# A transformer trunk's first feed-forward: its first two column groups interleaved by quarters of x, and the transfers of x set between those of the weights

## The chip, the cores and the metric

One core of a Trainium2 chip runs the whole program. The metric is the device time of one execution in microseconds; lower is better. TensorE (PE) does matrix products into the accumulation memory PSUM, with weight loads (PEld) beside them; VectorE (DVE), ScalarE (ACT) and GpSimd (POOL) work element by element; SyncE (SP) issues the transfers (DMA). Each engine works through its own queue in order.

## The reference

Two layers, each with a feed-forward, a mixing stage of three branches, and a second feed-forward. The change touches the first feed-forward of the first layer alone:

```python
def _swiglu(u, wi, wo):
    a, g = jnp.split(u @ wi, 2, axis=-1)
    return (jax.nn.silu(a) * g) @ wo

for l in range(DEPTH):
    x = x + 0.5 * _swiglu(_rms_norm(x, ffn1_norm[l]), ffn1_wi[l], ffn1_wo[l])
    ...
```

x has 256 tokens and 1024 features, `wi` is 1024 x 2816 and `wo` 1408 x 1024, all in float32.

## The kernel before

Every float32 operand is split into a high and a low part, and a product of two is done as three (high x high, high x low, low x high). For a weight tile, ACT casts the raw tile to the high part (`conv_hi`), and DVE subtracts it from the raw one for the low part (`conv_lo`). In the trace raw tiles are `raw`, and high and low parts are `whi` and `wlo` or, in another ring of buffers, two tiles `g`. There are four raw buffers (`RAW`); SP issues the transfer of a further tile where a low part has been issued and so releases a buffer.

The normalised x is used in a raw form first: x^T times the gain, as `uh` (high, ACT) and `ul` (low, DVE). The factor 1/rms of each token comes later, as a row `rrow` (`rows_of`). x arrives in four quarters of 256 features, two feature tiles of 128 each. In `first_norm` each quarter, in the trace `R`, is transposed on PE into an `at` tile (four products with the identity), and `raw_u` makes its two tiles of `uh` and then of `ul`.

The first feed-forward's up projection goes by column groups of 256 + 256 columns (`plan_ffn`): group c accumulates u @ wi over eight feature tiles k, with the weights of one group in tiles of one or two feature tiles. Such a group needs an accumulator of two PSUM banks (`big_ps`, kind `mm`); there are two of these. One feature tile is two units of six products (`feat_units`). When a group is done, `side_feat` multiplies the accumulator's first half by `rrow` (DVE), applies silu (ACT), multiplies by the accumulator's second half (DVE), gives the accumulator back, and splits the result.

The order of instructions is not written out. `drive` goes through the units in order; before each, `feed` issues weight casts and transfers, and `run_sides` advances the side works (`first_norm`, `side_feat`, and constants in `setup_late`), all by the estimates of `Flow`, which keeps a time for each engine. The engines' queues are then fixed, and semaphores hold them to the data.

The start of the program: in `setup` SP's queue gets quarter 0 of x, two weight tiles, quarter 1, a weight tile, quarter 2, a weight tile, quarter 3. PE does seven warm-up products on a tile of zeros, transposes quarter 0 and the gain, and does four more.

Of the kernel before, what the change touches and what calls it, by code (L numbers as in the profile page):

```python
# [18 lines left out]
P = 128  # L19
# [53 lines left out]
class WTile:  # L73
    """A weight tile: where it comes from, how it lies, and once loaded its hi and lo parts."""
# [8 lines left out]
class Flow:  # L83
    """Estimates when each engine is done with what it was given and when each piece of a tile is ready.

    Engines work in the order in which they are given instructions; the estimates choose that order, and
    the semaphores of the framework keep it right whatever the times turn out to be."""

    LAT, GRAN, COLD = 0.2, 64, 7.0
    TABLES = {AF.Exp: "natural_log_exp_and_others", AF.Ln: "natural_log_exp_and_others",  # L90
# [47 lines left out]
    def note(self, eng, op, args, kw):  # L138
        outs = [args[0]] + [kw[k] for k in ("accum_out",) if k in kw]
        ins = [x for x in (*args[1:], *(v for k, v in kw.items() if k != "accum_out")) if hasattr(x, "tensor")]  # L140
        start, known = self.t[eng], []
# [12 lines left out]
        if eng == "d":  # L154
# [3 lines left out]
            end = max(start, issue + 1.0) + size / 360e3  # L158
# [43 lines left out]
class Trunk:  # L202
    TAIL = 5
    RING, XRING, RAW, WARM = 5, 4, 4, (7, 4)
# [55 lines left out]
    def take(self, kind, shape=None, dt=F32):  # L260
        """a tile of a kind that is given back by hand"""
# [32 lines left out]

    def hook(self, u, *gens):
        self.hooks.setdefault(u, []).extend(gens)

# [7 lines left out]
    def able(self, since, wait):  # L305
        """wait: an engine ("p", "a", "v") and tiles that it reads, (kind, n) for slots, conditions, a time"""
# [32 lines left out]

    def dma_tile(self, i):  # L340
        w = self.tiles[i]
        w.raw = self.tile(self.wp, [P, 1024], "raw", self.RAW)
# [16 lines left out]
    def feed(self, u, urgent=False):  # L359
        """convert weight tiles ahead of unit u as the engines have time, and fetch further ones."""  # L360
# [37 lines left out]
    def drive(self):  # L398
        self.live, self.pend, self.nconv = {"m": [], "x": []}, [], 0
        for u, (w, emit, post, need, reads) in enumerate(self.units):  # L400
            for g in self.hooks.get(u, ()):
                self.spawn(g)
# [19 lines left out]
    def setup(self, N):  # L422
# [20 lines left out]
        for n in range(4):  # L443
            ns = slice(n * 256, (n + 1) * 256)
            nc.sync.dma_start(xt[:, :, ns], a["x"][0, :, ns].rearrange("(t p) c -> p t c", p=P))
            for _ in range((2, 1, 1, 0)[n]):
                self.dma_tile(self.ndma)
                self.ndma += 1
# [14 lines left out]
    def first_norm(self, N, xt, grow, pw, warm_up):  # L463
        nc = self.nc
# [1024 lines left out]
```

## Time and profile before

| | us |
|---|---|
| timed executions, median of 3 (lowest to highest) | 831.48 (831.39 to 831.77) |
| span of the profiled execution, first to last instruction | 829.8 |
| PE busy | 822.6 (99%) |
| DVE busy | 585.0 (70%) |
| ACT busy | 453.7 (55%) |
| share of PE in the chain that ended last | 98% |

The page gives no time of its own for the profiled execution beside the span; the timed executions are 1.7 us longer than it. Times in the rows below count from the span's start. A row of the timeline merges instructions of one kind: where it begins, how long the merged stretch is, how many there are (x4), and in brackets how long the engine was idle before and what ended that. Busy shares of PE are close to full nearly everywhere, since the ends of products are modelled; idle time on PE is read from the brackets and from the distance between starts.

### The profile page before, as it was taken

The numbers are of one execution on the slowest core, as the hardware profiler recorded it, in microseconds if no ns is written. First come the engines' busy times: TensorE is split into PE (matmuls) and PEld (weight loads), VectorE is DVE, ScalarE is ACT, GpSimd is POOL, SyncE is SP. The second block draws the span as 40 slices with busy tenths as digits, with TensorE's granted clock in tenths as the row PEclk, the third lists the DMA queues.
The fourth block names the chain that finished last, engine by engine and source line by source line (L and its number), as shares of the span: only waits on it lengthen the run. The fifth ranks groups of instructions, "written<-read, shape, count | busy, mean of one in ns | idle before, by whom it ended". The sixth has DMA issues, their size and how long they took to land.

```text
span 829.8 us, 16152 instructions
## 1 busy us (share of the span) xinstructions
PE 822.6 (99%) x6459; PEld 793.3 (96%) x6459; DVE 585.0 (70%) x939; ACT 453.7 (55%) x720; POOL 34.7 (4%) x49
## 2 busy tenths in 40 slices
PE   8999999999999999999999999999999999999998
PEld 6999999898999999999999999998989999999996
DVE  5787878987757488855775567898957475886541
ACT  6456545557775446644654444565676745655430
POOL 0000010200300000000000000101002000000000
PEclk9999999999999999999999999999999999999999
DMA  8678735643265746865567555366423655477521
GB/s 259 184 244 256 240 103 158 184 148 103 85 201 155 247 155 205 275 186 172 172 212 203 177 159 165 98 208 185 138 82 115 222 174 186 158 240 242 182 69 51
DMA packets 122255, 145.15 MB, mean 175 GB/s; under 512 B 7534, under 2 KB 97084, under 8 KB 122180
## 3 DMA queue, kind: packets, MB, share of 16 engines
q1 hardware_dynamic: 122020, 144.05, 56.2%
q8 instruction: 50, 0.82, 0.4%
q14 instruction: 25, 0.20, 0.1%
q10 hardware_dynamic: 160, 0.07, 0.0%
HBM read 143.05 MB, written 1.05 MB: 174 GB/s over the span
## 4 chain that ended last, share of the span: by engine, by line
PE 98%; DMA 1%; SPq 0%; DVE 0%; issue 0%
PE mm L188 65%; PE at L188 33%; DMA R<-in_x_dram 1%; DMA raw<-in_ffn_wi_dram 0%; SPq L188 0%; DVE xn L188 0%
## 5 line engine op out<-in xcount | busy, mean ns | idle before, releaser
L188 ACT CAST whi<-raw 128x1024 fp32r<-128x1024 f32 (+3 forms) x185 | 189.9, 1034 | 159.9 <-PE mm L188 58.5
L188 DVE TENSOR_TENSOR wlo<-raw,whi 128x1024 fp32r<-128x1024 f32 (+3 forms) x185 | 220.1, 1199 | 73.9 <-ACT whi L188 73.0
L188 PE MATMUL mm<-uh,whi 128*128 128x256 f32 x840 | 240.2, 286 | 0.0
L188 PE MATMUL mm<-uh,wlo 128*128 128x256 f32 x840 | 236.9, 282 | 0.0
L188 PE MATMUL mm<-ul,whi 128*128 128x256 f32 x840 | 236.4, 281 | 0.0
L188 PEld LDWEIGHTS mm<-ul,whi 128*128 128x128 f32 x840 | 158.8, 189 | 0.1
L188 PEld LDWEIGHTS mm<-uh,whi 128*128 128x128 f32 x840 | 158.0, 188 | 0.5 <-issue 0.3
L188 PEld LDWEIGHTS mm<-uh,wlo 128*128 128x128 f32 x840 | 157.9, 188 | 0.0
L188 PE MATMUL mm<-uh,g 128*128 128x256 f32 x752 | 138.9, 282 | 0.0
L188 ACT CAST g<-raw 128x1024 fp32r<-128x1024 f32 (+3 forms) x87 | 88.2, 1018 | 90.1 <-PE mm L188 35.3
L188 DVE TENSOR_TENSOR g<-raw,g 128x1024 fp32r<-128x1024 f32 (+3 forms) x87 | 102.4, 1183 | 22.4 <-ACT g L188 22.2
L188 PEld LDWEIGHTS mm<-uh,g 128*128 128x128 f32 x752 | 117.5, 188 | 0.0
L188 PE MATMUL mm<-ul,g 128*128 128x256 f32 x376 | 105.6, 281 | 0.0
L188 PE MATMUL at<-R,whi 128*128 128x256 f32 x404 | 71.9, 280 | 0.0
L188 PEld LDWEIGHTS mm<-ul,g 128*128 128x128 f32 x376 | 70.9, 188 | 0.0
L188 PE MATMUL at<-R,g 128*128 128x256 f32 x570 | 69.8, 280 | 0.0
L188 PEld LDWEIGHTS at<-R,g 128*128 128x128 f32 x570 | 68.2, 188 | 0.0
L188 PEld LDWEIGHTS at<-R,whi 128*128 128x128 f32 x404 | 61.6, 188 | 0.0
L188 PE MATMUL at<-R,wlo 128*128 128x256 f32 x202 | 56.3, 279 | 0.0
L188 PEld LDWEIGHTS at<-R,wlo 128*128 128x128 f32 x202 | 38.1, 189 | 0.0
L188 DVE TENSOR_TENSOR R<-s2k,R 128x512 fp32r<-128x512 f32 (+1 forms) x24 | 15.5, 647 | 25.7 <-ACT R L188 25.7
L188 PE MATMUL mm<-whi,uh 128*128 128x512 f32 (+1 forms) x76 | 30.0, 394 | 0.0
(229 smaller groups left out, 1150.0 us busy)
## 6 DMA issues: line engine op xcount, KB each, us to landing
raw<-in_w_in_dram SPq DMA_DIRECT2D x92, 512.0 KB
raw<-in_ffn_wi_dram SPq DMA_DIRECT2D x174, 256.0 KB
raw<-in_ffn_wo_dram SPq DMA_DIRECT2D x35, 512.0 KB
raw<-in_w_out_dram SPq DMA_DIRECT2D x16, 512.0 KB
raw<-in_ffn_wo_dram SPq DMA_DIRECT2D x12, 384.0 KB
raw<-in_w_up_ml_dram SPq DMA_DIRECT2D x16, 256.0 KB
raw<-in_w_in_dram SPq DMA_DIRECT2D x8, 424.0 KB
raw<-in_w_up_sb_dram SPq DMA_DIRECT2D x8, 256.0 KB
```

What stands on the lines that cost most here:

```text
L188: f(*args, **kw)
```

## The change

In the first feed-forward of the program, groups 0 and 1 are planned together: for each quarter of x, the four units of group 0 on it and then the four units of group 1 (`reorder`). All later groups are as before. The transfers of x are put before given weight tiles (`X_BEFORE`): quarter 0 ahead of tile 0, quarter 1 ahead of tile 3, quarter 2 ahead of tile 4, quarter 3 ahead of tile 5; those ahead of tiles 4 and 5 are thus issued when these tiles are. A quarter's transposes wait until the plan is at unit 8q - 3, that is, after the first of group 1's units on the quarter before. In quarter 0 the second feature tile of `uh` and `ul` waits for the first weight cast. Two warm-up products take the place of four, and the estimates take a lower rate for the first transfers. (The file also loses its comments, which shifts its line numbers.)

```diff
@@ class Flow @@
+    FIRST_RATE, FIRST_US = 240e3, 12.0
...
-            end = max(start, issue + 1.0) + size / 360e3
+            end = max(start, issue + 1.0) + size / (self.FIRST_RATE if issue < self.FIRST_US else 360e3)
@@ class Trunk @@
-    RING, XRING, RAW, WARM = 5, 4, 4, (7, 4)
+    RING, XRING, RAW, WARM = 5, 4, 4, (7, 2)
+    X_BEFORE = {0: 0, 3: 1, 4: 2, 5: 3}
...
+    def reorder(self, units):
+        self.units, self.tiles = [], []
+        for w, *_ in units:
+            w.first = None
+        for x in units:
+            self.unit(*x)
...
+    def dma_x(self, n):
+        ns = slice(n * 256, (n + 1) * 256)
+        self.nc.sync.dma_start(self.xt[:, :, ns], self.a["x"][0, :, ns].rearrange("(t p) c -> p t c", p=P))
+
     def dma_tile(self, i):
         w = self.tiles[i]
+        if i in self.X_BEFORE:
+            self.dma_x(self.X_BEFORE[i])
...
         for u, (w, emit, post, need, reads) in enumerate(self.units):
+            self.at_unit = u
@@ setup @@
-        for n in range(4):
-            ns = slice(n * 256, (n + 1) * 256)
-            nc.sync.dma_start(xt[:, :, ns], a["x"][0, :, ns].rearrange("(t p) c -> p t c", p=P))
-            for _ in range((2, 1, 1, 0)[n]):
-                self.dma_tile(self.ndma)
-                self.ndma += 1
+        self.xt = xt
+        for _ in range(self.RAW):
+            self.dma_tile(self.ndma)
+            self.ndma += 1
@@ first_norm @@
         for q in range(4):
+            yield lambda: self.at_unit >= 8 * q - 3,
             yield "p", xt[:, :, 256 * q:256 * q + 256], self.ident, ("ps", 1)
...
             yield "a", pt
-            self.raw_u(N, q, v)
+            if q == 0:
+                self.raw_u(N, q, v, (0,))
+                yield lambda: self.nconv > 0,
+                self.raw_u(N, q, v, (1,))
+            else:
+                self.raw_u(N, q, v)
@@ plan_ffn @@
-        for c in range(5):
+        start, c0 = not self.units, 0
+        if start:
+            c0, parts = 2, []
+            for c in range(2):
+                box = {}
+                first = len(self.units)
+                self.feat_units(tiles(256 * c, 256, (0, 1, 2, 4, 6, 8) if c == 0 else (0, 2, 4, 6, 8)), 4, U, box,
+                                lambda b=box, c=c: self.spawn(side_feat(b, 2 * c, 2)), key="n")
+                parts.append(self.units[first:])
+            self.reorder([x for q in range(4) for p in parts for x in p[4 * q:4 * q + 4]])
+        for c in range(c0, 5):
             box = {}
-            cuts = (0, 1, 2, 4, 6, 8) if not self.units else (0, 2, 4, 6, 8)
-            self.feat_units(tiles(256 * c, 256, cuts), 4, U, box,
+            self.feat_units(tiles(256 * c, 256, (0, 2, 4, 6, 8)), 4, U, box,
                             lambda b=box, c=c: self.spawn(side_feat(b, 2 * c, 2)), key="n")
```

How this moves instructions is shown at three places.

**DVE at the program's start.** Names: `at` an x quarter transposed, `gain` the norm's gain, `g` with an odd first number a weight tile's low part (written from the raw tile and the high part). Before:

```order
L188 COPY gain_20_116<-mm_17_106 128x8
L188 SCALAR_TENSOR_TENSOR ul_115<-at_21_117,gain_20_116,uh_114 128x256 x2
L188 TENSOR_TENSOR g_1_24_138<-raw_87,g_0_23_137 128x512
L188 TENSOR_TENSOR g_3_27_145<-raw_90,g_2_26_144 128x512
L188 SCALAR_TENSOR_TENSOR ul_115<-at_22_132,gain_20_116,uh_114 128x256 x2
L188 TENSOR_TENSOR g_5_31_163<-raw_94,g_4_30_162 128x1024
L188 SCALAR_TENSOR_TENSOR ul_115<-at_32_171,gain_20_116,uh_114 128x256 x2
L188 TENSOR_TENSOR g_7_35_191<-raw_98,g_6_34_190 128x1024
```

Now, where `g_7_35` and `g_3_42` are group 0's low parts for quarters 1 and 2, and `g_5_29` and `g_1_38` group 1's for quarters 0 and 1:

```order
L189 COPY gain_20_114<-mm_17_104 128x8
L189 SCALAR_TENSOR_TENSOR ul_113<-at_21_115,gain_20_114,uh_112 128x256 x2
L189 TENSOR_TENSOR g_1_23_127<-raw_87,g_0_22_126 128x512
L189 TENSOR_TENSOR g_3_25_130<-raw_90,g_2_24_129 128x512
L189 TENSOR_TENSOR g_5_29_145<-raw_93,g_4_28_144 128x1024
L189 SCALAR_TENSOR_TENSOR ul_113<-at_33_183,gain_20_114,uh_112 128x256 x2
L189 TENSOR_TENSOR g_7_35_189<-raw_97,g_6_34_188 128x1024
L189 TENSOR_TENSOR g_1_38_218<-raw_136,g_0_37_217 128x1024
L189 SCALAR_TENSOR_TENSOR ul_113<-at_40_254,gain_20_114,uh_112 128x256 x2
L189 TENSOR_TENSOR g_3_42_260<-raw_141,g_2_41_259 128x1024
```

A quarter's two `ul` still stand ahead of the low part that is used with them, and between the quarters there are now two low parts where there was one.

**ACT at the program's start.** `uh` and the casts of weight tiles (`g` with an even first number), before:

```order
L188 ACTIVATE uh_114<-at_21_117,gain_20_116 128x256 x2
L188 CAST g_0_23_137<-raw_87 128x512
L188 CAST g_2_26_144<-raw_90 128x512
L188 ACTIVATE uh_114<-at_22_132,gain_20_116 128x256 x2
L188 CAST g_4_30_162<-raw_94 128x1024
```

Now:

```order
L189 ACTIVATE uh_112<-at_21_115,gain_20_114 128x256
L189 CAST g_0_22_126<-raw_87 128x512
L189 CAST g_2_24_129<-raw_90 128x512
L189 ACTIVATE uh_112<-at_21_115,gain_20_114 128x256
L189 CAST g_4_28_144<-raw_93 128x1024
L189 CAST g_6_34_188<-raw_97 128x1024
L189 ACTIVATE uh_112<-at_33_183,gain_20_114 128x256 x2
```

The second `uh` of quarter 0 moved behind two casts, and quarter 1's pair behind the casts of two further tiles. In the same way quarter 3's pair stands behind the cast of the tenth tile, `raw_273`, whose transfer waits for the low part `g_3_42` to release its buffer.

**DVE where groups 0 and 1 are read out.** Names: `s2k_498` and `s2k_500` are the results of groups 0 and 1, `mm_30` and `mm_32` their accumulators, `rrow` the row of 1/rms, `consts_bf`, `sel`, `tri` and `posf` constants and positions. Before, with `mm_29` and `s2k_341` of group 0:

```order
L188 TENSOR_TENSOR g_5_55_314<-raw_177,g_4_54_313 128x1024
L188 TENSOR_TENSOR s2k_341<-mm_29_155,rrow_325 128x512
L188 TENSOR_TENSOR g_7_65_344<-raw_194,g_6_64_343 128x1024
L188 TENSOR_TENSOR s2k_341<-s2k_341,mm_29_155 128x512
L188 TENSOR_TENSOR g_1_68_354<-raw_256,g_0_67_353 128x1024
```

Now:

```order
L189 TENSOR_TENSOR s2k_498<-mm_30_147,rrow_486 128x512
L189 TENSOR_TENSOR s2k_500<-mm_32_176,rrow_486 128x512
L189 CAST consts_bf_77<-consts_72 128x128
L189 CAST consts_bf_77<-t_0_56_356 128x384
L189 CAST sel_74<-qk_55_353 8x512
L189 CAST tri_75<-consts_72 128x128
L189 CAST posf_508<-pos_358 128x2
L189 TENSOR_TENSOR s2k_498<-s2k_498,mm_30_147 128x512
L189 TENSOR_TENSOR s2k_500<-s2k_500,mm_32_176 128x512
```

The second multiplication, which is the last to read group 0's accumulator, moved behind five casts that stood after group 1's read-out before. On PE the third group's first product writes that accumulator again (`mm_94` has the buffer of `mm_30`) and stands right behind group 1's last products and the transposed constants.

## Rows read from the trace of the kernel before

**Rows 1.** The page: PE's granted clock in 40 slices, and the chain that ended last.

```profile
PEclk9999999999999999999999999999999999999999
...
PE 98%; DMA 1%; SPq 0%; DVE 0%; issue 0%
```

**Rows 2.** Timeline of PE from the start: start, length, line, operation, out<-in, count, [idle before].

```profile
1.09 3.17 PE L188 MATMUL mm<-s2k 128*128 128x512 bf16 x7 [1.09 <-POOL mhalf L188]
...
5.57 1.02 PE L188 MATMUL mm<-s2k 128*128 128x512 bf16 x4 [0.26 <-DVE gain L188]
7.41 0.66 PE L188 MATMUL at<-consts,R 128*128 128x128 f32 x4 [0.82 <-DMA R<-in_x_dram]
7.83 0.36 PE L188 MATMUL mm<-uh,g 128*128 128x256 f32 x1
...
10.46 0.66 PE L188 MATMUL at<-consts,R 128*128 128x128 f32 x4 [0.97 <-DMA R<-in_x_dram]
...
12.70 0.66 PE L188 MATMUL at<-consts,R 128*128 128x128 f32 x4 [0.17 <-DMA R<-in_x_dram]
13.11 0.36 PE L188 MATMUL mm<-uh,g 128*128 128x256 f32 x1
...
13.43 0.40 PE L188 MATMUL mm<-uh,g 128*128 128x256 f32 x2
...
20.53 0.40 PE L188 MATMUL mm<-uh,g 128*128 128x256 f32 x2
```

**Rows 3.** Timeline of ACT in the first 30 us.

```profile
5.55 0.84 ACT L188 ACTIVATE uh<-at,gain 128x256 fp32r<-128x256 f32 x2 [2.48 <-DVE gain L188]
6.28 1.14 ACT L188 CAST g<-raw 128x512 fp32r<-128x512 f32 x2
...
9.69 1.04 ACT L188 CAST g<-raw 128x1024 fp32r<-128x1024 f32 x1 [0.74 <-DMA raw<-in_ffn_wi_dram]
...
13.39 0.84 ACT L188 ACTIVATE uh<-at,gain 128x256 fp32r<-128x256 f32 x2 [0.40 <-PE at L188]
14.12 0.63 ACT L188 ACTIVATE s2k<-R 128x512 f32<-128x512 f32 x1
...
18.94 1.57 ACT L188 COPY x<-at 128x512 f32<-128x512 f32 x3
...
21.71 2.00 ACT L188 CAST g<-raw 128x1024 fp32r<-128x1024 f32 x2
...
29.27 1.06 ACT L188 CAST whi<-raw 128x1024 fp32r<-128x1024 f32 x1 [0.47 <-DMA raw<-in_ffn_wi_dram]
```

**Rows 4.** Timeline of DVE in the first 25 us.

```profile
6.42 0.88 DVE L188 SCALAR_TENSOR_TENSOR ul<-at,gain,uh 128x256 fp32r<-128x256 f32 x2 [0.91 <-ACT uh L188]
7.21 1.28 DVE L188 TENSOR_TENSOR g<-raw,g 128x512 fp32r<-128x512 f32 x2
...
17.66 0.16 DVE L188 SCALAR_TENSOR_TENSOR rcol<-ss 128x2 f32<-128x2 f32 x1
...
19.38 0.48 DVE L188 TENSOR_SCALAR dlo<-consts,rlo 128x128 fp32r<-128x128 f32 x2
19.77 1.22 DVE L188 TENSOR_TENSOR g<-raw,g 128x1024 fp32r<-128x1024 f32 x1
...
22.63 0.69 DVE L188 TENSOR_TENSOR s2k<-mm,rrow 128x512 f32<-128x512 f32 x1
...
24.36 0.68 DVE L188 TENSOR_TENSOR s2k<-s2k,mm 128x512 f32<-128x512 f32 x1
```

**Rows 5.** Timeline of SP's queue at 25 us: a weight tile's second half, the first constants.

```profile
24.89 0.47 SPq L188 DMA_DIRECT2D raw<-in_ffn_wi_dram  x1
25.40 0.41 SPq L188 DMA_DIRECT2D rows<-in_b_in_dram  x1
```

**Rows 6.** Timeline of DVE at 37 us: the first and the last of five casts.

```profile
36.88 0.22 DVE L188 CAST consts_bf<-consts 128x128 bf16<-128x128 f32 x1
...
37.76 0.15 DVE L188 CAST posf<-pos 128x2 f32<-128x2 int32 x1
```

More of the change, by code (lines that the diff above doesn't have):

```diff
@@ L594, in new_u, with raw_u @@
         N["n"] = N["m"] = 0
-    def raw_u(self, N, q, src):
+    def raw_u(self, N, q, src, js=(0, 1)):
         nc = self.nc
-        for k in (2 * q, 2 * q + 1):
+        ks = [2 * q + j for j in js]
+        for k in ks:
             nc.scalar.activation(N["h"][:, k], src[:, k % 2], AF.Copy, scale=N["gain"](k))
-        for k in (2 * q, 2 * q + 1):
+        for k in ks:
             nc.vector.scalar_tensor_tensor(N["l"][:, k], src[:, k % 2], N["gain"](k), N["h"][:, k].bitcast(F32),
```

## Prediction

> **What bounds the kernel now.** I read three views of the profile in this order. The chain of waits first: nearly all of it is TensorE (PE) [rows 1], so a time saved or lost elsewhere counts only where PE waits for it. Then PE's timeline from the start [rows 2]. It makes warm-up products until 6.6 us, waits 0.82 us for the second quarter of x, does 12 products, waits 0.97 us for the third quarter, does 12 more, waits 0.17 us for the fourth, and from 13.11 on no row has a wait before it. The sixty products between 13.43 and 20.53 start 0.118 us apart; this is PE's pace. Then ScalarE (ACT) and VectorE (DVE) in the same stretch [rows 3, 4], for what stands before each product: an x quarter is transposed on PE, scaled by ACT (uh), its remainder taken by DVE (ul); a weight tile is cast by ACT and its remainder (the low part) taken by DVE.
>
> To compare the two orders I ask as from when PE would have worked without a gap. Before, at 12.70, it has done 24 products and two sets of transposes (0.41 us each, 12.70 to 13.11): 24 x 0.118 + 2 x 0.41 = 3.65, so "as from" 9.05. All PE work after that is the same in both kernels apart from its order.
>
> **The change, term by term.** Each term is a place where PE waits in the new order.
>
> 1. *The first products: -0.45 us.* The transposes of quarter 0 and uh of feature tile 0 (5.55) stay. Of the first products, the third needs the low part g_1. On DVE g_1 now stands behind both ul, and the second ul needs the second uh, which ACT now does after two casts. ACT: uh at 5.55; half a pair (0.84) takes it to about 5.92; two casts of 512 columns, 0.52 apart (1.14 for two), the second not before its weights are there. Those were there at 6.80 at the latest (the second cast of the pair from 6.28 [rows 3]) and possibly earlier; I take 6.7. So uh at 7.2, ready 7.68; ul at 7.7; g_1 0.4 later (two ul and then g_1: 6.42 to 7.21 is 0.79 [rows 4]), at 8.1, ready after 0.68 at 8.8; third product at 8.84. With two products behind it that is "as from" 8.60: 0.45 earlier than 9.05. If the cast waits for nothing but ACT it is 8.34, if until 6.80 8.71: -0.7 to -0.35. The two warm-up products less (0.5 us) lie in the wait.
>
> 2. *Quarter 1: +0.83.* PE does 22 more products (to 11.44); the weight tile of group 1 was landed at the latest when the same bytes had landed before (9.69), its cast and low part need 0.95 + 1.22 us, ready by 10.9 to 11.9, no wait or a short one. Six products of group 1, then quarter 1's transposes at 12.14. From there PE has 0.41 + 18 products + 2 of the next = 2.77 us of work until it needs g_7, the low part of the next tile. On DVE g_7 stands behind both ul of the quarter: transposes to uh 0.69 (12.70 to 13.39), pair of uh 0.84, two ul 0.79, low part 1.22, some 0.06 for the hand-overs: 3.6 us. PE waits 3.6 - 2.77 = 0.83. Before, the same chain ran beside 24 to 48 queued products.
>
> 3. *Quarter 2: +0.83.* The same order once more: transposes at 19.05, PE ready at 21.82, the low part g_3 at 22.65.
>
> 4. *Quarter 3: +0.8.* Transposes at 25.96; the second next product of group 0 is due at 28.6 and needs ul. On ACT uh now stands behind a cast whose tile is fetched into the buffer that g_3 releases, at 22.65. In the trace a tile whose second half was issued at 24.89 [rows 5], the first 0.41 before, was cast at 29.27 by an ACT that had waited 0.47 for it [rows 3]: 4.8 us; some other tile was quicker, I take 4.1 to 4.8, so it lands at 27.1 (26.75 to 27.45). Cast 0.95, uh pair 0.84, ul 0.5: 29.4. Wait 0.8 (0.45 to 1.15).
>
> 5. *The third column group: +3.5.* Its first product overwrites the accumulator (mm) of group 0. Before, DVE's last read of it ended at 25.05 [rows 4], 8 us before the third group began (13.11 + 168 products + 2 = 33.2), so nobody waited. Now groups 0 and 1 end together. PE is through with both at 29.4 + 23 + 24 + 3 products = 35.3. The read needs 1/rms in a row: four squares (0.63 each), four copies of x (0.5 each) and two casts (0.95 each) stand ahead of the row's copy on ACT, 28.8 + 2.5 + 2.0 + 1.9 = 35.2, copied at 35.55. (DVE's and GpSimd's part of 1/rms, 17.66 to 19.86 before, ends near 33.6 and is not the late one.) DVE multiplies group 0 and group 1 by the row (0.6 apart), then makes five small casts of constants (36.88 to 37.91 before [rows 6], 1.03), and only then the product with silu that frees the accumulator (0.68, as at 24.36): 35.55 + 1.2 + 1.03 + 0.69 = 38.5. The casts also wait for positions that were there at 37.76 at the latest; the small transfers now start some 0.45 later than at 25.40 [rows 5], as the tile ahead of them waits for a low part that ends near 24.85. That bounds it at 37.76 + 0.45 + 0.18 + 0.69 = 39.1. I take 38.8. Wait 3.5 (3.2 to 3.8).
>
> The Trainium skill ("Perfetto Trace Analysis", Optimizing Tensor Performance, Matmuls) speaks against this order: independent groups should rotate through PSUM banks, so that one group is read out while the next is multiplied. Before does so (read out at 22.63 to 25.05 beside the products of group 1), and by that rule alone the change costs the read-out, term 5.
>
> Sum: -0.45 + 0.83 + 0.83 + 0.8 + 3.5 = +5.5 us. The third group starts at 38.8 where it started at 33.3. Nothing later gives it back: the order of transfers from the sixth weight tile on is the same, and the chain of waits is PE's to the end. The page gives a span of 829.8; the timed runs, median 831.48, hold 1.7 more around it. 829.8 + 5.5 + 1.7 = **837.0 us**, 0.66% slower. Bounds: each term at its ends gives +4.2 to +6.2; the re-planned order up to the first mixing stage adds perhaps 0.5 either way. A measurement of this kernel can tell some 0.2% (1.7 us) from no change.
>
> **Rivals.**
>
> *The clock falls in a gap: 838.7.* The granted clock reads full throughout [rows 1], but the rows show both levels: seven warm-up products in 3.17 us (0.42 apart), four in 1.02 (0.22) [rows 2]. So PE came from 1.2 to 2.4 GHz between 4.3 and 5.6, 3.2 to 4.5 us after it began. Gaps of 0.82 and 0.97 us left the products after them at 0.118. The new order has longer ones: some 2.2 us between 6.1 and 8.84 with two products in it, and 3.5 us before the third group. If the clock falls in one, products start 0.21 apart instead of 0.118 for as long as it took at the start: 3.2 to 4.5 us x 0.44 = 1.4 to 2.0, say +1.7. No row shows a gap so long. The Trainium skill ("TensorE: Matmul & The Clock Gate", What's actually happening) says that half speed is the default and that activity releases it, which leans to this rival. Chance 0.2.
>
> *The accumulator is free in time: 833.5.* If the constants' casts or the row come much earlier, term 5 shrinks to what silu and its product need. It vanishes only if the read-out ends by 35.3, 3.5 us before my count; against it stands DVE's order, which is fixed. -0.45 + 0.83 + 0.83 + 0.8 = +2.0. Chance 0.08.
>
> *The delay is absorbed: 831.5.* If a later stage, the first mixing stage near 200 us, is paced by something that does not start later, a late PE loses nothing there. It decides if that stage waits at least 5.5 us for work that does not hang on PE. The chain of waits gives PE 98% and no such wait [rows 1]; but ends of products are modelled, so small waits could be hidden. Chance 0.06.
>
> *The change does as it is built to: 829.4.* Two groups per quarter give PE twice the work per byte of x. If g_1 were ready when its weights and the first uh are (first product near 6.6, third at 6.9, "as from" 6.7) and terms 2 to 5 were nothing, it would gain 2.3 us. It needs DVE to work out of its order. Chance 0.04.
>
> **How the numbers follow.** My forecast has the remaining 0.62. Range 834.8 to 838.9: the forecast with its bounds and most of the clock rival; outside lie the three others (0.18) and the far end of the clock. Slower by over 0.2%: 0.62 + 0.2 + 0.08 = 0.90; within 0.2%: 0.06; faster: 0.04.
>
> **What would show it.** Right: PE's third product at 8.6 to 9.0; idle rows before PE near 15, 22 and 29 of 0.4 to 1.2 us, released by DVE; an idle row of 3 to 4 us near 35 to 39, released by DVE's product with silu; the third group at 38.3 to 39.2. Wrong: no idle row at the third group (accumulator rival); products 0.21 apart after a gap (clock rival); a third group that starts 5 us later and an end that does not (absorbed).

## The result and the profile after

The changed kernel takes 844.74 us (median of 4, 843.67 to 845.70); the kernel before, measured beside it, takes 831.43 us (831.06 to 831.77). The ratio is 1.0159, 95% interval 1.0145 to 1.0174: 13.3 us slower. Forecast were 837.0 us with a range of 834.8 to 838.9. The sign was right, the size was not; 844.74 lies outside the range.

The profiled execution of after took 845.7 us and its span is 843.4 us, 13.6 more than before's 829.8. The page of after, PE's granted clock in 40 slices and the chain that ended last, beside [rows 1]:

```profile
PEclk9989999999999999999999999999999999999999
...
PE 95%; DMA 3%; SPq 1%; DVE 1%; ACT 0%; issue 0%; ACTq 0%; DVEq 0%
```

The third slice is 42.2 to 63.3 us: a slice with less than full clock. The chain leaves PE for 5% of the span. What PE waited for (sum, times, longest):

```profile
PE mm L189 <- DVE s2k L189: 5.0, 1, 5.0
PE mm L189 <- DVE g L189: 2.4, 3, 1.2
...
PE at L189 <- DVE xn L189: 0.4, 1, 0.4
```

PE's timeline, answering to [rows 2] (columns as there):

```profile
5.83 1.01 PE L189 MATMUL mm<-s2k 128*128 128x512 bf16 x2 [0.26 <-DVE gain L189]
...
8.86 0.80 PE L189 MATMUL mm<-uh,g 128*128 128x256 f32 x2 [1.22 <-DVE g L189]
...
10.31 0.63 PE L189 MATMUL mm<-uh,g 128*128 128x256 f32 x2
10.73 0.41 PE L189 MATMUL mm<-ul,g 128*128 128x256 f32 x1
...
14.23 0.60 PE L189 MATMUL at<-consts,R 128*128 128x128 f32 x4
...
17.81 0.50 PE L189 MATMUL mm<-uh,g 128*128 128x256 f32 x2 [0.61 <-DVE g L189]
...
24.80 0.50 PE L189 MATMUL mm<-uh,g 128*128 128x256 f32 x2 [0.61 <-DVE g L189]
...
28.22 0.60 PE L189 MATMUL at<-consts,R 128*128 128x128 f32 x4
...
36.71 0.25 PE L189 MATMUL at<-consts,rows 103*128 103x103 f32 x1
41.94 0.55 PE L189 MATMUL mm<-uh,g 128*128 128x256 f32 x1 [4.98 <-DVE s2k L189]
...
42.50 0.63 PE L189 MATMUL mm<-uh,g 128*128 128x256 f32 x2
42.93 0.41 PE L189 MATMUL mm<-ul,g 128*128 128x256 f32 x1
```

Lengths overlap, so the pace is read from the distances between starts. The three products at 10.31 and 10.73 take until 10.95, 0.213 us apiece, and so do those at 42.50 and 42.93: the lower of the clock's two levels (1.2 GHz). Nineteen products between 9.24 and 13.08 and 24 between 42.29 and 47.20 start 0.213 apart; the other products in this stretch start 0.118 apart, but for a first one behind a wait or behind transposes.

ACT, answering to [rows 3], and SP's transfer of the tile that is cast at 28.39 (its first half):

```profile
5.82 0.47 ACT L189 ACTIVATE uh<-at,gain 128x256 fp32r<-128x256 f32 x1 [2.74 <-DVE gain L189]
6.19 1.13 ACT L189 CAST g<-raw 128x512 fp32r<-128x512 f32 x2
...
28.39 1.05 ACT L189 CAST g<-raw 128x1024 fp32r<-128x1024 f32 x1 [2.62 <-DMA raw<-in_ffn_wi_dram]
...
36.32 0.41 ACT L189 COPY rrow<-at 128x256 f32<-128x256 f32 x1
```

```profile
24.82 0.37 SPq L189 DMA_DIRECT2D raw<-in_ffn_wi_dram  x1
```

DVE ahead of the third column group, answering to [rows 4, 6], and SP's first constants, answering to [rows 5]:

```profile
37.38 1.28 DVE L189 TENSOR_TENSOR s2k<-mm,rrow 128x512 f32<-128x512 f32 x2
38.58 0.22 DVE L189 CAST consts_bf<-consts 128x128 bf16<-128x128 f32 x1
40.31 0.36 DVE L189 CAST consts_bf<-t 128x384 bf16<-128x384 f32 x1 [1.51 <-DMA t<-in_consts_dram]
...
41.13 1.27 DVE L189 TENSOR_TENSOR s2k<-s2k,mm 128x512 f32<-128x512 f32 x2
```

```profile
27.97 1.08 SPq L189 DMA_DIRECT2D rows<-in_b_in_dram  x3
...
36.76 0.35 SPq L189 DMA_DIRECT2D t<-in_consts_dram  x1
```

The mechanism of term 5 stands there: casts, one of which waits 1.51 us for the transfer of `t`, and only then (41.13) the product with silu that frees the accumulator.

From the later part of the first mixing stage on, PE does the same work in the same order in both kernels. The chain of waits, start, length and what, at the first pieces of the mixing stage and behind it, and in a later down-projection; after and then before:

```profile
158.68 16.86 PE mm L189 x72
...
277.44 23.02 PE mm L189 x192
...
392.65 37.21 PE at L189 x312
```

```profile
147.40 16.86 PE mm L188 x72
...
265.23 23.04 PE mm L188 x192
...
380.06 36.68 PE at L188 x312
```

Between the first two of these after takes 118.76 us and before 117.83. The third is a stretch of 312 products with nothing between them: 119.3 ns a product against 117.6. The prediction had no term for this.

Where the 13.6 us are, from these rows:

| stretch | us | forecast |
|---|---|---|
| first products and the waits for the low part in quarters 1 and 2 (terms 1 to 3) | +1.2 | +1.2 |
| low clock until 13.1 (19 products x 0.095 = 1.8) and what is left of the stretch up to 36.71 | +2.3 | 0 |
| quarter 3 (term 4) | 0 | +0.8 |
| wait for the accumulator (36.71 to 41.94, less one product) | +5.1 | +3.5 |
| low clock behind that wait (24 x 0.095) | +2.3 | 0 (a rival: +1.7) |
| first mixing stage (118.76 less 117.83) | +0.9 | 0, 0.5 either way |
| slower products in five long stretches of the down-projections | +1.8 | 0 |

### The profile page after: what moved, and what is told of

The parts are those of the page before. It is cut to its first block, busy times and chain, and to the rows that moved or that the text cites. A ratio compares the mean times of both kernels' runs of the same rounds, so it can differ in the third digit from the quotient of the medians.

```text
span 843.4 us, 16148 instructions
## 1 busy us (share of the span) xinstructions
PE 830.3 (98%) x6457; PEld 799.7 (95%) x6457; DVE 583.9 (69%) x939; ACT 454.0 (54%) x720; POOL 34.4 (4%) x49
## 4 chain that ended last, share of the span: by engine, by line
PE 95%; DMA 3%; SPq 1%; DVE 1%; ACT 0%; issue 0%; ACTq 0%; DVEq 0%
PE mm L189 62%; PE at L189 33%; DMA raw<-in_ffn_wi_dram 2%; SPq L189 1%; DMA t<-in_consts_dram 0%; DMA consts<-in_consts_dram 0%; DVE g L189 0%; ACT g L189 0%; DVE ul L189 0%; DVE xn L189 0%; DVE s2k L189 0%; ACT uh L189 0%; DVE sel L189 0%; DVE consts_bf L189 0%; DVE tri L189 0%
## 5 line engine op out<-in xcount | busy, mean ns | idle before, releaser
L189 PE MATMUL mm<-uh,g 128*128 128x256 f32 x752 | 144.1, 288 | 7.4 <-DVE s2k L189 5.0
L189 PEld LDWEIGHTS mm<-uh,g 128*128 128x128 f32 x752 | 121.3, 194 | 9.2 <-issue 5.2
L189 PE MATMUL mm<-ul,g 128*128 128x256 f32 x376 | 107.6, 286 | 0.0
L189 PE MATMUL at<-R,whi 128*128 128x256 f32 x416 | 75.5, 283 | 0.0
L189 PEld LDWEIGHTS mm<-ul,g 128*128 128x128 f32 x376 | 73.2, 195 | 0.0
L189 PE MATMUL at<-R,g 128*128 128x256 f32 x552 | 67.9, 281 | 0.0
L189 PEld LDWEIGHTS at<-R,g 128*128 128x128 f32 x552 | 66.5, 188 | 0.0
L189 PEld LDWEIGHTS at<-R,whi 128*128 128x128 f32 x416 | 64.8, 192 | 0.0
L189 PE MATMUL at<-R,wlo 128*128 128x256 f32 x208 | 58.8, 283 | 0.0
L189 PEld LDWEIGHTS at<-R,wlo 128*128 128x128 f32 x208 | 39.9, 192 | 0.0
```

What stands on the lines that cost most here:

```text
L189: f(*args, **kw)
```

## The experiments

Each kernel was timed beside the kernel before; the ratio is to that one (after: 1.0159). Every kernel computes the whole; a kernel's name begins with a if it is an edit of after, with b if of before.

| kernel | us | ratio, 95% interval | third group starts | products 0.213 apart: start, behind the gap |
|---|---|---|---|---|
| after | 844.74 | 1.0159 (1.0145 to 1.0174) | 41.94 | 19, 24 |
| a_warm6 | 841.66 | 1.0117 (1.0101 to 1.0133) | 39.41 | 0, 13 |
| a_warmp | 842.83 | 1.0122 (1.0094 to 1.0149) | 39.99 | 5, 20 |
| a_fill | 843.18 | 1.0133 (1.0116 to 1.0150) | 43.05 | 20, 0 |
| a_late | 841.27 | 1.0111 (1.0094 to 1.0127) | 39.85 | 21, 15 |
| a_silu | 841.87 | 1.0105 (1.0076 to 1.0134) | 40.09 | 15, 15 |
| a_two | 837.46 | 1.0065 (1.0052 to 1.0078) | 37.69 | 26, 0 |
| a_ahead | 837.82 | 1.0076 (1.0061 to 1.0091) | 37.08 | 14, 0 |
| a_oldx | 838.66 | 1.0092 (1.0077 to 1.0107) | 37.27 | 12, 0 |
| a_place | 842.53 | 1.0130 (1.0113 to 1.0147) | 41.03 | 17, 27 |
| a_pad | 843.39 | 1.0143 (1.0128 to 1.0158) | 42.10 | 14, 20 |
| b_warm2 | 831.56 | 0.9998 (0.9989 to 1.0007) | not read | 10, 0 |
| b_pad | 833.68 | 1.0019 (1.0011 to 1.0028) | not read | 0, 0 |
| b_newx | 833.86 | 1.0031 (1.0019 to 1.0042) | not read | 0, 0 |
| d5 | 830.40 | 0.9983 (0.9973 to 0.9992) | 31.86 | 0, 0 |

### The clock at the start

```diff
-    RING, XRING, RAW, WARM = 5, 4, 4, (7, 2)
+    RING, XRING, RAW, WARM = 5, 4, 4, (7, 6)
```

> The changed kernel with six warm-up products behind the first transposes instead of two; they lie in the wait for the first low part and are in nobody's way. In the trace of after, products from 8.86 to 12.9 us start 0.213 apart instead of 0.118: about 19 products x 0.095 = 1.8 us. Theory (the clock was late because PE had little to do between 5.6 and 8.9): the clock is up by about 9, quarter 1's transposes come at 12.3 instead of 14.2, and the kernel is 1.5 to 2.0 us faster than after (842.9 for 844.7). Rival (the clock rises at a moment of its own, whatever PE does, or the lost time is made up at the third column group, which waits for DVE): products may start 0.118 apart earlier, the third group still starts at 41.5 to 42, and the total stays within 0.5 us of after.

No product was slow at the start, the third group began 2.5 us earlier, and the kernel came to 841.66. But the planner, told of the four products, also put the first low part ahead of the second ul on DVE, and the third product came at 7.44 instead of 8.86: two edits in one. So a second kernel hid the four products from the planner; every other instruction keeps its place:

```diff
-        wb = warm.bitcast(BF16)
+        wb = self.wb = warm.bitcast(BF16)
...
                 warm_up(self.WARM[1])
+                for _ in range(4):
+                    nc.tensor.eng.matmul(pw[:, 0], lhsT=self.wb[:, 0:P], rhs=self.wb[:, 0:512], start=True, stop=True)
```

> The changed kernel with four more warm-up products behind the first transposes; the planner is not told of them, so that every other instruction on every engine stays in its place (in the kernel with six warm-ups known to the planner DVE also made the first low part ahead of the second ul, which moved the third product from 8.86 to 7.44). Theory (the clock alone): no products 0.213 apart behind 8.9, quarter 1's transposes at 12.3 to 12.5 instead of 14.23, the third column group 1.8 to 2.2 us earlier, at about 40; the idle row before it and the slow products behind it stay. Rival (that gain came from DVE's order): slow products until 13 as in after, no gain.

PE's timeline:

```profile
6.67 1.91 PE L499 MATMUL mm<-s2k 128*128 128x512 bf16 x4
...
13.03 0.60 PE L189 MATMUL at<-consts,R 128*128 128x128 f32 x4
...
39.99 0.55 PE L189 MATMUL mm<-uh,g 128*128 128x256 f32 x1 [4.18 <-DVE s2k L189]
```

The four warm-ups are themselves slow (0.42 apart), then five products are, then none: the clock is up near 10.3 instead of 13.1. Quarter 1's transposes come 1.2 us earlier (the expectation had 1.8), the third group 1.95 earlier. The 1.2 us are the clock's, with every other instruction in its place, and they reach the third group: DVE's products with the row of 1/rms begin 1.14 us earlier. So the start is on the path, though PE waits 4 to 5 us later on: the chain that it waits for there (x's quarters, ACT, the row of 1/rms, DVE) starts from PE's transposes. The other 0.8 us are the transfer of `t`, which held DVE 0.71 us here instead of 1.51, and one trace can't put them down to the clock: in a_place and a_pad (below), where PE, DVE, ACT and SP have their instructions in the order of after, it held DVE 0.57 and 1.78 us, and the third group began at 41.03 and 42.10. The timed runs give 1.9 us, with intervals that just overlap.

The same order of instructions does not fix the clock at the start either. The two warm-ups of after start 0.38 apart, those of a_pad 0.21:

```profile
6.08 0.59 PE L189 MATMUL mm<-s2k 128*128 128x512 bf16 x2 [0.26 <-DVE gain L189]
```

There the clock was up, and it fell behind an idle row of 1.53 us. Either way products behind them are slow, 19 and 14.

In the kernel before:

```diff
-    RING, XRING, RAW, WARM = 5, 4, 4, (7, 4)
+    RING, XRING, RAW, WARM = 5, 4, 4, (7, 2)
```

> The kernel before with two warm-up products behind the first transposes instead of four, as after has it. In before the clock is up by 5.6 us; in after, whose PE did the same until 5.3, it came only at 13. Theory (the two products less keep it down): products of quarter 0 start 0.213 apart, the twelve between 7.8 and 9.2 end 1.1 us later, partly in the wait for quarter 1 of x; up to 1 us slower, 832 to 832.5. Rival (the clock rises at a moment that has nothing to do with them): as before, 831.2 to 831.7.

The two warm-ups ran fast, so two less did not keep the clock down as the theory had it; but then PE waited 1.43 us for x, and the ten products behind that were slow. The time did not change (0.9998): the wait for the next quarter of x, 0.97 us in before, is gone. So the theory had the slow products and the rival the time. In all ten profiles with two warm-ups there some of the first products are slow (10 to 26); in the three with four (before, b_pad, b_newx) and in a_warm6 and d5 with six none is; a_warmp, also with six, has five.

### The accumulator and DVE's order

```diff
-                self.hook(u0 + 21, self.setup_late())
+                self.hook(u0 + 40, self.setup_late())
```

> The changed kernel with the constants' transfers and casts started 19 units (about 13 us) later, so that they don't stand ahead of the product with silu on DVE. Theory (term 5: the third column group waits for an accumulator which DVE's queue of casts holds): in after the casts cost 38.58 to 41.13, of it 1.5 us waiting for a transfer; without them the first product with silu begins at about 38.8 and the third group starts at 39.4 instead of 41.94, 2.5 us earlier. If the clock also stays up in the shorter gap (2.4 us) another 2.3 us: 4.8 in all, 839.9. If it falls as before: 842.2. Rival (the accumulator is not what it waits for, the weights are): the third group starts as in after and the time stays at 844.7.

```profile
39.85 0.36 PE L189 MATMUL mm<-uh,g 128*128 128x256 f32 x1 [2.70 <-DVE s2k L189]
```

The third group at 39.85, 2.1 us earlier, and 15 slow products instead of 24 behind a gap of 2.70 us: 841.27, between the two numbers expected. Here the transfers of the constants are later as well. To part the two, only the casts were held back, until groups 0 and 1 have given back their accumulators (`freed` counts these):

```diff
-        yield "v",
+        yield "v", (lambda: self.freed > 1)
         nc.vector.tensor_copy(self.cb[:, 0, :], self.ident)
...
             self.give(box["pp"])
+            self.freed += 1
```

> The changed kernel in which the five casts of constants on DVE wait, in the plan, until groups 0 and 1 have given back their accumulators: on DVE both products with silu now stand ahead of the casts, on SP nothing moves. Theory (term 5: what holds the third group is DVE's order, whose casts also wait for the transfer of t): the first product with silu at 39.0, the third group at 39.8 instead of 41.94; slow products behind the gap as long as the clock falls in one of 2.7 us (it did in the kernel with the later constants, 15 products, 1.4 us): 2.1 + 0.9 = 3 us faster than after. Rival (the gain of that other kernel came from the transfers, which were later there): third group at 41.5 or later.

DVE's timeline:

```profile
37.82 1.28 DVE L189 TENSOR_TENSOR s2k<-mm,rrow 128x512 f32<-128x512 f32 x2
39.26 1.28 DVE L189 TENSOR_TENSOR s2k<-s2k,mm 128x512 f32<-128x512 f32 x2 [0.16 <-ACT s2k L189]
40.46 0.22 DVE L189 CAST consts_bf<-consts 128x128 bf16<-128x128 f32 x1
```

The third group starts at 40.09 (39.8 expected) in a run whose PE was 0.35 late by then. SP issues the transfers as in after (that of `t` at 36.69, there at 36.76), and they hold nobody now: it is DVE's order that lets them delay PE. What is left of the wait, 2.7 us, is the read-out itself. The next kernel takes away the accumulator: the third group goes into two of the four `at` buffers.

```diff
             if "pp" not in box:
...
+                if self.at_unit == 32:
+                    box["pp"] = box["ps"] = [self.main_ps() for _ in range(2)]
+                    box["vs"] = [t.rearrange("p (m c) -> p m c", m=2) for t in box["ps"]]
+                    box["at"] = lambda m: box["vs"][m // 2][:, m % 2, :]
...
```

> The changed kernel with the third column group accumulated in two buffers of the transposes (at) instead of the pair of banks (mm) that group 0 used; everything else is as the planner then orders it. Theory (the third group waits only for the accumulator, and the clock falls because of that wait): no idle row near 37, the third group starts near 37 instead of 41.94, no products 0.213 apart behind it: 5.0 + 2.3 us faster than after, 837.4. Rival (weights or x's copies would make it wait anyway, or the wait moves to the fourth group): an idle row of 2 us or more near 37 or near 60, 840 or more.

```profile
37.66 0.25 PE L189 MATMUL at<-consts,rows 103*128 103x103 f32 x1
37.69 0.37 PE L189 MATMUL at<-uh,g 128*128 128x256 f32 x1
```

No wait, no slow product behind it, 837.46 for 837.4 expected. The third group starts at once, though DVE reads group 0 out only from 38.34 on: it was the accumulator that it waited for. From the constants' product to the thirtieth product behind it after takes 11.17 us (36.71 to 47.88) and a_two 3.55 (37.66 to 41.21), so the wait and the clock behind it are worth 7.6 us here, where the rows of after give 5.1 + 2.3. That the total fits so closely is in part luck: planned anew, a_two loses 0.95 us more ahead of that product, with 26 slow products at the start, and gains 0.4 later on. The Trainium skill ("Perfetto Trace Analysis", Optimizing Tensor Performance, Matmuls) asks for independent groups to rotate through banks of PSUM so that one is read out while the next is multiplied. With the third group in other banks this trace agrees, at 7.6 us.

What if the gap stays and only PE's idleness goes? In `feat_units`:

```diff
+                if self.at_unit == 32:
+                    pf = self.main_ps()
+                    for _ in range(38):
+                        self.nc.tensor.eng.matmul(pf[:, 0:S], lhsT=U["h"][:, 0, 0:P], rhs=U["h"][:, 0], start=True, stop=True)
+                    self.give(pf)
                 box["pp"] = self.big_ps() if nm == 4 else self.main_ps()
```

> The changed kernel with 38 products that nobody reads, into a buffer of the transposes, put in PE's queue between group 1 and the third column group, where PE idles 4.98 us. At 0.118 each they fill 4.5 us. Theory (the clock falls because of that gap): the third group still starts near 41.9, now with products 0.118 apart at once, where after has 24 products 0.213 apart: 2.3 us faster than after, 842.4. Rival (the products behind the gap are slow for another reason, weights or the accumulator's bank): they stay 0.213 apart with filler ahead of them, no gain.

The filler ran from 36.90 at 0.12 us apiece, 1.36 us of the gap were left, and no product behind it was slow: it was the gap that let the clock fall. But the cast of `t` began 1.1 us later in this kernel (41.42) and the third group at 43.05, so that of 2.3 us 1.2 were left by the trace and 1.6 by the timed runs (843.18 for 842.4 expected). That transfer differs from kernel to kernel: from its issue to the cast it took 4.55 us here, 3.55 in after, 3.24 in a_place and 4.44 in a_pad, though DVE, ACT and SP have one order of instructions in all four. Why is open.

The last one goes back to terms 2 and 3:

```diff
-            yield lambda: self.at_unit >= 8 * q - 3,
+            yield lambda: self.at_unit >= 8 * q - 5,
```

> The changed kernel with the transposes of each quarter of x five units ahead of their first product instead of three; nothing else by hand. Theory (terms 2 and 3: PE waits for the low part behind both ul): the waits of 0.61 us near 18 and 25 go, each quarter comes that much earlier, and with quarter 3 the row of 1/rms and so the third column group: it starts near 40.5, and the time is 1.2 to 1.8 us less, 843 to 843.5. Rival (the third group hangs on transfers that don't move): it starts near 41.9 with a longer idle row before it, 844.5 to 845.

```profile
18.69 0.60 PE L189 MATMUL at<-consts,R 128*128 128x128 f32 x4
...
37.08 0.36 PE L189 MATMUL mm<-uh,g 128*128 128x256 f32 x1 [2.11 <-DVE s2k L189]
```

The waits of 0.61 went, as terms 2 and 3 say (quarter 2's transposes come 6.13 us behind quarter 1's, where after takes 7.00), but the time fell by 7 us, not by 1.5: with other estimates the planner put the product with silu ahead of the casts on DVE by itself, and behind a gap of 2.11 us the clock stayed up. The expectation forgot that every edit of this plan plans DVE anew.

### The order of transfers

```diff
-    X_BEFORE = {0: 0, 3: 1, 4: 2, 5: 3}
+    X_BEFORE = {0: 0, 2: 1, 3: 2}
...
         for _ in range(self.RAW):
             self.dma_tile(self.ndma)
             self.ndma += 1
+        self.dma_x(3)
```

> The changed kernel with the column groups in the new order but all quarters of x transferred as early as in before. Theory (the cost lies in the order of the products: waits for DVE, the accumulator, the clock behind it, the buffers' places): still over 842, an idle row of 4 to 5 us before the third group. Rival (it lies in the order of transfers): at most 838.

With x as early as in before: 838.66, the third group at 37.27 behind an idle row of 1.85. Neither number was met. Again DVE's order had flipped, the product with silu (36.45) ahead of the casts (40.15). What this shows is that after's casts in front of that product are no consequence of the new order of products as such, but of estimates that a small change tips over; what the transfers cost by themselves it doesn't show.

In the kernel before, the loop over x in `setup` gives way to that of after, and `dma_tile` gets its x:

```diff
+    X_BEFORE = {0: 0, 3: 1, 4: 2, 5: 3}
...
         w = self.tiles[i]
+        if i in self.X_BEFORE:
+            n = self.X_BEFORE[i]
+            ns = slice(n * 256, (n + 1) * 256)
+            self.nc.sync.dma_start(self.xt[:, :, ns], self.a["x"][0, :, ns].rearrange("(t p) c -> p t c", p=P))
...
```

> The kernel before, column groups one after the other as they were, with only the order of transfers changed: x's quarters 1, 2 and 3 between those of the weights as in after. Theory (this order is for two groups a quarter; one group alone needs the next quarter after 12 products): PE waits longer for quarters 1 and 2 than the 0.82 and 0.97 us of before; 1 to 2 us slower, 832.5 to 833.5, and by more if the clock falls in such a wait. Rival (these waits are set by something else than the order): 831.2 to 831.8.

```profile
43.04 0.39 PE L188 MATMUL mm<-uh,g 128*128 128x256 f32 x1 [0.95 <-ACT g L188]
...
44.30 0.50 PE L188 MATMUL mm<-uh,g 128*128 128x256 f32 x2 [0.75 <-DVE g L188]
```

With the groups one after the other (the planner moves a few products and casts) the new order of transfers takes 833.86 us, 2.2 to 2.6 us more than before. That is close to the theory's number, but not by its mechanism. PE waits 0.45 us for x, where before waits 1.96, and 0.36 and 0.50 us for weights, and it comes to the constants' product at 34.01, before at 34.02: up to there nothing is lost. The 2.2 us are lost at 43 us, in the third column group, where PE waits 0.95 us for the cast and 0.75 us for the low part of a weight tile and starts slowly behind both.

### The places of the buffers

In `take`, the buffers that before makes behind the last `g4` buffer are made there too; no instruction moves:

```diff
+        if kind == "g4" and i == 7 and "ss" not in self.ring:
+            self.sb([P, 2, 2], "ss")
...
+            self.sb([P, 8, S], "R2", dt=F32R)
+            self.sb([P, 3, S], "R3", dt=F32R), self.sb([P, 3, S], "R4", dt=F32R)
```

> The changed kernel with every instruction as it is; only the buffers of the hidden activations (R2, R3, R4) and the small ones made beside them are put at the addresses in SBUF that they have in before (in after they lie 6880 bytes further). Theory (the products of the down-projections start 119.9 ns apart in after against 117.7 in before because of where their operands lie): back to 117.7, some 1.4 to 1.9 us less in four down-projections, 843.0. Rival (it comes from the later time, transfers or other engines beside them): 119.9 stays, no change.

The chain of waits:

```profile
391.26 36.68 PE at L189 x312
```

36.68, exactly as before. So the 0.5 us in each such stretch hang on addresses alone. Which property of them?

```diff
-                H["ah"], H["al"] = self.sb([P, 8, S], "R1", dt=F32R), self.sb([P, 8, S], "R2", dt=F32R)
+                H["ah"] = self.sb([P, 8, S], "R1", dt=F32R)
+                if "pad1" not in self.ring:
+                    self.sb([P, 8], "pad1")
+                H["al"] = self.sb([P, 8, S], "R2", dt=F32R)
                 H["bh"], H["bl"] = self.sb([P, 3, S], "R3", dt=F32R), self.sb([P, 3, S], "R4", dt=F32R)
+                if "pad2" not in self.ring:
+                    self.sb([P, 8], "pad2")
```

> The changed kernel with every instruction as it is and one empty buffer of 32 bytes ahead of R2, so that R2, R3 and R4 lie at multiples of 64 bytes as in before, but not at the addresses of before. Theory (multiples of 64 decide): products of the down-projections 117.7 ns apart as in before, 842.6 to 843.2. Rival (the distances to other buffers decide): some other value than 117.7; 119.9 would be no change, 844.7.

> The kernel before with every instruction as it is and one empty buffer of 32 bytes ahead of R2, which moves R2, R3 and R4 by 32 bytes; a second one behind R4. In after these three lie at addresses that 64 does not divide, in before at ones that it does; R1 lies 32 past a multiple of 64 in both. Theory (that alone makes the products of the down-projections 119.9 ns apart instead of 117.7): 119.9 here, 1.4 to 2.0 us slower than before, 833.2. Rival (it is some other distance between buffers): 117.7 stays, no change.

The same 32 bytes in after (first fence) and in before (second):

```profile
391.87 36.68 PE at L189 x312
```

```profile
381.17 37.05 PE at L188 x312
```

They cure after and harm before. The timed runs say it of before (1.0019, 1.6 us slower); of after they give 1.3 us, which its interval can't tell from nothing, and the trace 2.0 us over the five long stretches. Worked out from the traces for all 1176 products that stream R1 to R4, the mean distance to the next start is 117.6 to 117.7 ns in six kernels with R2 at a multiple of 64 bytes (before, a_place, a_pad, b_warm2, b_newx, d5) and 118.9 to 119.3 in the nine with R2 32 bytes past one (after, a_warm6, a_warmp, a_fill, a_silu, a_two, a_ahead, a_oldx, b_pad). One doesn't fit: a_late has R2 at a multiple of 64, at another place, and 118.6. Multiples of 64 are most of it, not all; what the rest is stays open. R1 lies 32 bytes past a multiple of 64 in all sixteen, so whether R2's own address counts or its place against R1's was not tested.

### All of it together

> The changed kernel with all that the runs so far point to: six warm-up products at the start, buffers at the addresses of before, the third column group in two buffers of the transposes, the constants' casts 19 units later, and the transposes of each quarter of x five units ahead of their first product instead of three, so that the low part behind both ul is done in time (waits of 0.6 to 1.1 us near 15, 18 and 22 in the runs so far). Theory: the first two groups end near 33 and the third begins there as in before (33.3); with 0.9 us more in the first mixing stage the time is 830.5 to 832, no difference from before that can be told, 13 us better than after. Rival (something in this order costs time that none of these parts takes away): 834 or more.

d5 joins the edits of a_warm6, a_two, a_late, a_ahead and a_place. PE's waits over the whole program and the start of the third group:

```profile
PE mm L189 <- POOL mhalf L189: 1.1, 1, 1.1
PE mm L189 <- DVE gain L189: 0.3, 1, 0.3
PE at L189 <- DMA R<-in_x_dram: 0.2, 1, 0.2
PE mm L189 <- DVE g L189: 0.2, 1, 0.2
```

```profile
31.86 0.36 PE L189 MATMUL at<-uh,g 128*128 128x256 f32 x1
```

830.40 us, 0.9983 of before (0.9973 to 0.9992): 14.3 us under after, 1.4 under before by the ratio, and just under what was expected (830.5 to 832). Before waited 0.82, 0.97 and 0.17 us for x [rows 2]; here PE waits for 0.4 us in all once it has its gain (the 1.1 us are ahead of its first product). That is what the change gives with these five edits beside it, and it is close to the 829.4 of the prediction's last rival.

## Why the prediction was right and wrong

**Terms 1 to 3 were right, term 1 in part by luck.** The third product was counted for 8.84 and came at 8.86. But uh began at 5.82, 0.27 later than counted, and the second cast, for which the count let ACT wait some 0.26 us, followed the first without a wait (6.19): two errors that cancel. From quarter 1's transposes to quarter 2's, PE took 7.00 us where 6.91 were counted, and 6.99 to quarter 3's: a wait of 0.61 by the bracket, 0.77 from start to start, where 0.83 stood. The two sums along DVE (3.6 us) and PE (2.77 us) hold, and a_ahead, which gives PE two units more, has no such wait.

**Term 4 was wrong: 0 instead of 0.8.** The chain is as told, but the transfer in it was mis-sized. It was issued at 24.82, as g_3 ended, and the cast on its tile ran at 28.39: 3.6 us, where 4.1 to 4.8 stood, taken from one row of before. PE was 2.3 us late itself, but that changes nothing, for this chain hangs on PE's transposes and was late with it. Counted from quarter 3's transposes ul was ready 1.0 us earlier than reckoned, 0.8 of it by the transfer: it ended at 30.70, and PE came to it at 30.90.

**The clock is the step that failed first.** It was one rival at 0.2 with a price of 1.7 us, for one gap; the forecast itself put it at nothing. The rows of after have it twice, 1.8 us at the start and 2.3 us behind the gap. At the start it was no gap's doing: the clock was not up yet when PE made its two warm-ups (1.01 us for two, where before made four in 1.02), a case that no rival had. The working said that gaps of 0.82 and 0.97 had left the clock up [rows 2] and that no row showed a longer one; it then left full clock as the default for gaps of 2.2 and 3.5 us, at odds of four to one, with nothing behind these odds. In full work the runs show the clock falling behind idle rows of 2.70 to 5.25 us (seven profiles) and staying up behind 1.85 and 2.11 (two); at the start, behind two warm-ups, it was down after 1.43 (b_warm2). It need not fall within the gap: in a_late the first ten products behind it still start 0.118 apart, and the slow ones begin at 41.17. And the price at the start was thought to be PE's alone, where it shifts each later step: in a_warmp, 1.2 us faster on PE by quarter 1, DVE reads the accumulators out 1.14 us earlier. The Trainium skill ("TensorE: Matmul & The Clock Gate", What's actually happening) has half speed as the default and activity as what releases it. That leaned to this rival; the prediction said so and then gave it too little.

**Term 5 had the mechanism and was undersized: 5.1 instead of 3.5.** The order on DVE and the chain to the row of 1/rms are as told (the row's copy began at 36.32, 1.1 us behind the count of 35.2, with PE 1.5 us late by then; DVE took the row up 0.65 us after it was there, behind two small operations that the count left out). What failed is the bound on the constants' transfers: "some 0.45 later than at 25.40". SP started them at 27.97, 2.57 later, since the tile ahead of them waited for a low part that ended at 27.02, not at 24.85; so `t` was issued at 36.76, and its cast could begin at 40.31, 3.55 us later, where 2.78 us were enough in before (34.24 to 37.02). The other queue on which the end of the wait hung was bounded from a single row. a_silu and a_late show 2.3 us of after's wait to be the casts (1.3 to 2.6 beside a_place and a_pad, whose waits are 4.04 and 5.25), and a_two that the accumulator is all of it.

**What lay beyond the planning stretch was wrong too.** "Nothing later gives it back" holds, but something later adds to it: 0.9 us in the mixing stage, of it 0.4 in one new wait (DVE xn), which goes where the stage is planned anew (a_ahead, a_silu, d5) and so is an accident of that plan; and 1.8 us by addresses. The prediction compared the order of instructions and not where the buffers lie. With the clock (2.3 + 2.3), term 5 (+1.6) and term 4 (-0.8) set right, the sum would have come to 842.4; the last 2.7 us of the profile (0.9 + 1.8) were not to be had from the part of the trace that was read.

**The rivals.** The accumulator in time, the delay absorbed, the change as built: all three were wrong for this kernel, as their chances said. The third of them comes within 1 us of what d5 takes: its condition, DVE out of PE's way, is what d5's edits make, with two things that the rival did not have, warm-ups for the clock and other banks for the third group.

## What to carry to other kernels

When an order is made by a planner, price the change by the queue of the engine that frees a buffer, row by row, and bound each transfer in front of it from the queue that issues it and from the buffer that it waits for, not from one row shifted by a guess: from the issue of one transfer to the cast on it passed 3.2 to 4.6 us in four kernels with the same queue. A gap on PE can cost more than its length (here 2.3 us more for one of 5.0): read the distances between starts behind it. And where later stages have the same instructions but other durations, compare the addresses of their operands before looking for a cause in time.

## What the runs showed of the hardware

- *Half speed under a column that reads full.* In after the granted clock reads 1.00 from 10 to 15 us, where products start 0.213 apart up to 13.1; from 40 to 45 it reads 0.56. Windows of after (stretch, its length, PE busy and instructions, clock, DMA share, GB/s):

```profile
10.00:15.00 5.00, 5.00 (x32) 1.00 1.04 343
40.00:45.00 5.00, 3.06 (x14) 0.56 0.92 294
45.00:50.00 5.00, 5.00 (x35) 0.76 0.58 176
```

  In a_two and b_warm2, whose warm-ups ran fast before the clock fell, the column does show the fall (0.50 and 0.84 from 10 to 15). In these traces the column shows nothing of the clock until it has once been up; the distance between starts does.
- *Addresses in SBUF.* Moving three of the four activations by 32 bytes changed the pace of the 1176 products that stream the four, between 117.6 and 119.3 ns, with not one instruction changed: 1.6 us in before (b_pad, timed), 2.0 in after (1176 x 1.7 ns, from the traces of after and a_pad).
